# Second mixer's attention as 64-by-64 products on two column halves of TensorE

## The chip, the cores and the metric

The kernel runs on one core of one Trainium2 chip. The metric is the device time of one execution in microseconds. Beside it stands one profiled execution, whose instructions and their times are the trace. Engines are named as the profile does: PE is TensorE's matmuls, PEld its weight loads, DVE is VectorE, ACT is ScalarE, POOL is GpSimd, SP is SyncE, which issues the weight DMAs.

## What is computed

A trunk of two layers over 256 tokens of width 2048, all in float32. Layer 0 has an mLSTM mixer, layer 1 a bidirectional gated linear recurrence (HGRN2), each followed by a ConvGLU block. The change touches the recurrence of layer 1 alone. It has 16 heads of width 128; in one direction, and in chunks of 64 tokens, it is:

```python
def _hgrn_chunk(s_st, xs):
    q, k, lf, v = xs                        # (b, h, 64, 128); lf is the log of the gate
    b = jnp.cumsum(lf, axis=2)
    rel = jnp.where(lower[:, :, None], b[:, :, :, None, :] - b[:, :, None, :, :], -jnp.inf)
    attn = jnp.einsum('bhtsk,bhsk->bhts', jnp.exp(rel) * q[:, :, :, None, :], k)
    o = jnp.einsum('bhts,bhsv->bhtv', attn, v) + jnp.einsum('bhtk,bhkv->bhtv', q * jnp.exp(b), s_st)
    ...
y = hgrn_direction(q, k_f, lf_f, v) + fl(hgrn_direction(fl(q), fl(k_b), fl(lf_b), fl(v)))
```

Written without chunks, the weight of token s in the output at token t is the sum over 128 channels of q[t] k[s] and the product of the gates of all tokens between them, with the forward gates where s is before t and the backward ones where it is after.

## The kernel before

**The stream of weights.** Everything runs under one loop, `stream`, over chunks of weight columns. `split_weights` loads a piece of weights (`raw`), ScalarE rounds it to `wh` (L145), VectorE subtracts the rest into `wl` (L146), and TensorE multiplies: feature-major chunks with weights as the stationary operand (L196 with 512 moving columns, L197 with 256), token-major chunks with the tokens stationary (L186 to L188, 512 columns each). The cast of a piece runs three pieces ahead (`LOOK`). After each step the loop calls `side.tick`, which advances the jobs beside the stream: generators that issue a few instructions and then yield the modelled time until their next turn. The heads of both mixers are such jobs. The order in which the instructions of each engine finally stand is chosen by a scheduler at build time, from this program.

**A head of the second mixer** (`head`, L595 to L656) builds the 256 by 256 matrix of weights between tokens by doubling. `QZ` and `KZ` hold q and k for both directions, with decay applied so far. At level h the tokens form blocks of 2h; within each, the product of the first half's keys with the second half's queries, and the other way round, is a pair (s, t) whose blocks of h differ and whose blocks of 2h agree. Seven levels, h = 1 to 64, cover all pairs within 128 tokens; one more product at the end covers the pairs between the two halves of 128 (L638, L639).

A visit of the job does one level:

- `gather` (L609, `km` and `qm`, four buffers each): VectorE brings the keys and queries that belong to this level into token order.
- L626: two float32 matmuls of 128x128x128 give `pd`, one for each half of the sequence. Only the pairs of this level in it are wanted. L616 is the same for the diagonal, with `ks` and `q`.
- `put` (L604): VectorE copies the wanted pairs with a 0/1 mask of 128 columns out of PSUM into the diagonal blocks of the result `AT`, which POOL has set to zero (L601).
- L627, L628: VectorE multiplies the level's blocks of keys and queries by the gates between them; POOL multiplies neighbouring gates for the next level (L633).

Each visit then yields `SPREAD` = 2.4 (`STEP` = 1.9 in the last two heads). After the last level, L651 multiplies `AT` by the values `V`, ScalarE takes the squares, and the job `finish` scales and transposes the head (L672) for the output projection.

In the first mixer, L393 and L394 transpose four blocks that lie on 64 partitions; the trace shows them as 64*128 where everything else shows 128*128.

Of the kernel before, what the change touches and what calls it, by code (L numbers as in the profile page):

```python
# [8 lines left out]
F32 = mybir.dt.float32  # L9
F32R = mybir.dt.float32r  # L10
I32 = mybir.dt.int32
AF = mybir.ActivationFunctionType
ALU = mybir.AluOpType
PSUM = bass.MemoryType.PSUM

P = 128
T = 256
# [6 lines left out]
BH = 16  # L24
# [15 lines left out]
STEP = 1.9  # L40
SPREAD = 2.4
# [3 lines left out]
MIX = 4  # L45
FIRST = (0, 1, 2, 4, 7, 10, 13, 16)

LEVELS = (1, 2, 4, 8, 16, 32, 64)
C_ID, C_MF, C_MB, C_LV = 0, 128, 384, 640
NCST = C_LV + len(LEVELS) * P  # L50


def trunk_kernel(ctx, tc, xT, pp_d, cst_d, w_first, w_aq, w_ak, w_av, w_ao, w_aout,
                 w_bq, w_bv, w_bg, w_bout, w_up, w_down, out, mscr, stop=9):
    nc = tc.nc
    act, dve, pool, pe = nc.scalar, nc.vector, nc.gpsimd, nc.tensor
# [7 lines left out]
    pp = keep.tile([P, NPP], F32, name="pp")  # L64
    cst = keep.tile([P, NCST], F32, name="cst")
    ones = keep.tile([P, T], F32, name="ones")
# [4 lines left out]
    ident = cst[:, C_ID:C_ID + P]  # L71
# [5 lines left out]
    def aux(name):  # L77
        return psa.tile([P, 512], F32, tag="aux", name=name)
# [132 lines left out]
    def fm_scaled(ps, R, dst, scale=None):  # L211
        fm_sum(ps, dst)
        if scale is None:
            dve.tensor_tensor(dst, dst, R, ALU.mult)
        else:
            dve.scalar_tensor_tensor(dst, dst, scale, R, ALU.mult, ALU.mult)
# [75 lines left out]
    def head_scale(ss, width):  # L292
        rs = ev.tile([P, 2], F32, tag="rs", bufs=6, name="rs")
        dve.tensor_scalar(rs, ss, 1.0 / width, EPS, ALU.mult, ALU.add)
        pool.tensor_tensor(rs, rs, hmx, ALU.pow)
        return rs
# [238 lines left out]
    def hgrn(norm, nxt):  # L535
# [24 lines left out]
        def blocks(z, h, a, b):  # L560
            v = z[:, 0:2 * (T + h)].rearrange("k (p x) -> k p x", p=2)[:, :, a:b]
            return v.rearrange("k p (m j) -> k m p j", j=2 * h)[:, :, :, 0:h]

        def gview(g, n, start, h):
            v = g[:, start:start + 2 * (n - 1)].rearrange("k (p x) -> k p x", p=2)[:, :, 0::2]
            return v.rearrange("k p m -> k m p").unsqueeze(3).broadcast_to([P, n // 2, 2, h])

        def take(hd, what, ps):
            mp = box["mp"]
            st = heads[hd]  # L570
            if what == 0:
                st["q"] = mp.tile([P, T], F32, tag="q", bufs=2, name="q")
                fm_scaled(ps, norm.R, st["q"], box["oml"][:, hd:hd + 1])
                st["QK"] = mp.tile([P, 1152], F32, tag="QK", bufs=2, name="QK")
                st["G"] = mp.tile([P, 768], F32, tag="G0", bufs=2, name="G")
                return
            dr = what - 1
            lb, oml = box["lb"], box["oml"]
            QZ, KZ, G = st["QK"][:, 0:512], st["QK"][:, 512:1024], st["G"]
            z = mp.tile([P, T], F32, tag="z", bufs=2, name="z")  # L580
            fm_scaled(ps, norm.R, z)
            g = G[:, dr * T:(dr + 1) * T]
            kz = KZ[:, dr * T:(dr + 1) * T]
            act.activation(g, z, AF.Sigmoid)
            act.activation(kz, z, AF.Sigmoid, scale=-1.0)
            dve.tensor_scalar(g, g, oml[:, hd:hd + 1], lb[:, hd:hd + 1], ALU.mult, ALU.add)  # L586
            pool.tensor_tensor(QZ[:, (1 - dr) * T:(2 - dr) * T], st["q"], g, ALU.mult)
            if dr == 0:
                pool.tensor_copy(G[:, 512:768], g)
            else:  # L590
                st["ks"] = mp.tile([P, T], F32, tag="ks", bufs=2, name="ks")
                pool.tensor_tensor(st["ks"], KZ[:, 0:T], KZ[:, T:2 * T], ALU.add)
                side.push(head(hd))

        def head(hd):  # L595
            mp = box["mp"]
            st = heads[hd]
            QZ, KZ = st["QK"][:, 0:640], st["QK"][:, 512:1152]
            q, ks, G = st["q"], st["ks"], st["G"]
            AT = mp.tile([P, 4, P], F32, tag="AT", bufs=2, name="AT")  # L600
            pool.memset(AT[:, 0::3], 0.0)  # L601

            def put(ps, mask):
                dve.copy_predicated(AT[:, 0::3], mask.bitcast(I32).unsqueeze(1).broadcast_to([P, 2, P]),  # L604
                                    ps[:, 0:T].rearrange("p (a b) -> p a b", a=2))

            def gather(z, h, tag):
                m = mp.tile([P, T], F32, tag=tag, bufs=MIX, name=tag)
                dve.tensor_copy(m.rearrange("k (m p j) -> k m p j", p=2, j=h), blocks(z, h, 0, T))  # L609
                return m  # L610

            km, qm = gather(KZ, 1, "km"), gather(QZ, 1, "qm")
            pd = aux("pd")
            for t in range(2):
                c = slice(t * P, (t + 1) * P)
                pe.matmul(pd[:, c], ks[:, c], q[:, c], start=True, stop=True)  # L616
            put(pd, ident)
            step = SPREAD if hd < BH - 2 else STEP
            yield step
            n = T  # L620
            for li, h in enumerate(LEVELS):
                pd = aux("pd")
                qa, ka = blocks(QZ, h, 0, T), blocks(KZ, h, 0, T)
                for t in range(2):
                    c = slice(t * P, (t + 1) * P)
                    pe.matmul(pd[:, c], km[:, c], qm[:, c], start=True, stop=True)  # L626
                dve.tensor_tensor(ka, ka, gview(G, n, 1, h), ALU.mult)  # L627
                dve.tensor_tensor(qa, qa, gview(G, n, n + 1, h), ALU.mult)  # L628
                if h < 64:
                    km, qm = gather(KZ, 2 * h, "km"), gather(QZ, 2 * h, "qm")  # L630
                    n //= 2
                    G2 = mp.tile([P, 3 * n], F32, tag=f"G{h}", bufs=2, name="G2")
                    pool.tensor_tensor(G2, G[:, 0:6 * n:2], G[:, 1:6 * n:2], ALU.mult)  # L633
                    G = G2
                put(pd, cst[:, C_LV + li * P:C_LV + (li + 1) * P])
                yield step
            pd = aux("pd")
            pe.matmul(pd[:, 0:P], KZ[:, 0:P], QZ[:, T + P:2 * T], start=True, stop=True)  # L638
            pe.matmul(pd[:, P:T], KZ[:, T + P:2 * T], QZ[:, 0:P], start=True, stop=True)  # L639
            act.copy(AT[:, 1:3], pd[:, 0:T].rearrange("p (a b) -> p a b", a=2))  # L640
            yield
            while "V" not in st["qd"]:
                yield
            V, j = st["qd"]["V"], hd % 4
            py = aux("py")
            y = mp.tile([P, T], F32, tag="y", bufs=4, name="y")
            ss = mp.tile([P, 2], F32, tag="ss", bufs=2, name="ss")
            for t in range(2):
                c = slice(t * P, (t + 1) * P)
                for s in range(2):  # L650
                    pe.matmul(py[:, c], AT[:, 2 * s + t], V[:, s, j * P:(j + 1) * P], start=(s == 0), stop=(s == 1))  # L651
            act.copy(y, py[:, 0:T])
            for t in range(2):
                jk = ev.tile([P, T], F32, tag="jk", bufs=1, name="jk")
                act.activation(jk[:, 0:P], y[:, t * P:(t + 1) * P], AF.Square, accum_out=ss[:, t:t + 1])
            st["y"] = (y, head_scale(ss, 128))  # L656
# [109 lines left out]
    if stop > 1:  # L766
        c, close0 = ffn(0, n1, n2)
        chunks += c
    if stop > 2:
        c = hgrn(n2, n3)  # L770
        b = c[0].before
# [6 lines left out]
    if stop > 3:  # L778
        c, close1 = ffn(1, n3, nf)
# [29 lines left out]
def _constants():  # L809
    c = np.zeros((P, NCST), np.float32)  # L810
    s, t = np.arange(P)[:, None], np.arange(P)[None, :]
    c[:, C_ID:C_ID + P] = s == t
    c[:, C_MF:C_MF + P] = np.where(s > t, BIG, 0.0)
    c[:, C_MB + P:C_MB + 2 * P] = np.where(s < t, BIG, 0.0)
    for i, h in enumerate(LEVELS):
        c[:, C_LV + i * P:C_LV + (i + 1) * P] = (s // (2 * h) == t // (2 * h)) & (s // h != t // h)
    return c


# [53 lines left out]
```

## Time and profile before

| | |
|---|---|
| median of 3 runs | 2469.81 us (2469.35 to 2470.11) |
| the profiled execution's own time | 2469.78 us |
| its span in the trace | 2468.0 us |
| granted TensorE clock, mean | 0.998 |
| second mixer's products, first to last start | 1146.7 to 1646.0 us |
| L626, 448 instructions | 276 ns mean, 66.4 us busy |
| L616, 64 instructions | 274 ns mean |
| L604, 128 masked copies | 436 ns mean, 55.5 us busy |
| POOL memsets of AT (L601), 16 | 314 ns mean |

A row of the groups names line, engine and operation, then output and inputs by the program's names, shapes and count, then busy time and mean duration of one, then the idle time of the engine just before them and what ended it. `128*128` are rows and columns of the array in use. Instructions of TensorE overlap: a duration runs from start to the modelled end, so the pace is read from the starts. One float32 matmul of the program is two weight loads and two matmul instructions in the trace. A timeline row has the start, the duration, the engine, the line and the form, and how many of a kind were merged.

### The profile page before, as it was taken

Reading aid. Unit: us, or ns where it says so; the run is one execution under the profiler, and the core shown is the slowest. Engines: PE = TensorE matmul, PEld = TensorE weight load, DVE = VectorE, ACT = ScalarE, POOL = GpSimd, SP = SyncE. Lnnn points to the kernel's source line nnn. Section 1 sums busy time; section 2 is a strip of 40 time slices with the busy share of each in tenths; the row PEclk is TensorE's granted clock in tenths of the full one; section 3 lists DMA queues with packets and bytes.
Section 4 is the critical chain, followed back from the end, with each engine's and each line's share of the span. In section 5 each row is a group of like instructions: output and inputs, shape, how many; then the busy total and the mean of one; then the engine's idle time right before and its main releaser. Section 6 shows DMA issues by size and latency. Waiting matters only on the chain.

```text
span 2468.0 us, 35972 instructions
## 1 busy us (share of the span) xinstructions
PE 2450.2 (99%) x13950; PEld 2134.1 (86%) x13950; DVE 1781.9 (72%) x2975; ACT 1200.8 (49%) x1810; POOL 272.8 (11%) x341
## 2 busy tenths in 40 slices
PE   9999999999999999999999999999999999999998
PEld 7888888888888888888888888888888888888887
DVE  7766577777656777678888888887777755677754
ACT  6655455444444445444444444445544444444443
POOL 0100032000000000132222222224000000000022
PEclk9999999999999999999999999999999999999999
DMA  7654555666556555555454544446555555666553
GB/s 260 189 178 167 177 183 188 190 189 191 186 189 199 188 188 189 180 194 178 157 168 154 164 161 156 163 145 202 187 189 188 188 188 190 192 192 193 183 190 124
DMA packets 65915, 449.07 MB, mean 182 GB/s; under 512 B 7616, under 2 KB 8128, under 8 KB 15568
## 3 DMA queue, kind: packets, MB, share of 16 engines
q1 hardware_dynamic: 63936, 443.29, 55.4%
q0 software_dynamic: 800, 2.16, 0.6%
q8 instruction: 109, 1.79, 0.3%
q10 hardware_dynamic: 1008, 1.32, 0.1%
q14 instruction: 62, 0.51, 0.1%
HBM read 444.58 MB, written 2.16 MB: 181 GB/s over the span
## 4 chain that ended last, share of the span: by engine, by line
PE 90%; DVE 7%; issue 1%; ACT 1%; DMA 0%; DVEq 0%; POOL 0%; POOLq 0%
PE mm L196 50%; PE mm L197 25%; PE mm L187 3%; PE mm L188 3%; PE mm L186 3%; DVE wl L146 3%; DVE QK L627 1%; PE pd L626 1%; DVE km L609 1%; PE pn L439 1%; PE mm L175 1%; DVE AT L604 1%; PE py L651 1%; DVE qm L609 1%; DVE G L586 0%
## 5 line engine op out<-in xcount | busy, mean ns | idle before, releaser
L146 DVE TENSOR_TENSOR wl<-raw,wh 128x1024 fp32r<-128x1024 f32 (+1 forms) x864 | 1047.1, 1213 | 553.6 <-ACT wh L145 540.6
L145 ACT CAST wh<-raw 128x1024 fp32r<-128x1024 f32 (+1 forms) x864 | 884.4, 1024 | 895.8 <-PE mm L196 500.4
L196 PE MATMUL mm<-xt,wh 128*128 128x512 f32 x3776 | 1318.5, 395 | 0.0
L197 PE MATMUL mm<-xt,wl 128*128 128x256 f32 x3776 | 1050.8, 278 | 0.0
L196 PEld LDWEIGHTS mm<-xt,wh 128*128 128x128 f32 x3776 | 708.0, 188 | 161.2
L197 PEld LDWEIGHTS mm<-xt,wl 128*128 128x128 f32 x3776 | 709.9, 188 | 0.9
L196 PE MATMUL mm<-g,wh 128*128 128x512 f32 x1334 | 462.6, 394 | 0.0
L197 PE MATMUL mm<-g,wl 128*128 128x256 f32 x1334 | 369.5, 277 | 0.0
L196 PEld LDWEIGHTS mm<-g,wh 128*128 128x128 f32 x1334 | 250.1, 188 | 58.1
L197 PEld LDWEIGHTS mm<-g,wl 128*128 128x128 f32 x1334 | 250.4, 188 | 0.0
L186 PE MATMUL mm<-wh,xt 128*128 128x512 f32 x512 | 203.9, 402 | 2.2 <-ACT xt L203 2.2
L187 PE MATMUL mm<-wl,xt 128*128 128x512 f32 x512 | 204.5, 399 | 0.4 <-DVE wl L146 0.4
L188 PE MATMUL mm<-wh,xt 128*128 128x512 f32 x512 | 201.9, 396 | 0.0
L208 ACT COPY b<-mm 128x256 f32<-128x256 f32 x237 | 87.7, 370 | 178.9 <-PE mm L197 178.9
L242 POOL TENSOR_TENSOR acc<-hx 128x256 f32<-128x256 f32 x4 | 4.8, 1205 | 1239.7 <-DVE hx L311 1239.7
L186 PEld LDWEIGHTS mm<-wh,xt 128*128 128x128 f32 x512 | 96.1, 189 | 21.0 <-ACT xt L203 2.5
L187 PEld LDWEIGHTS mm<-wl,xt 128*128 128x128 f32 x512 | 97.0, 189 | 18.4 <-DVE wl L146 0.8
L188 PEld LDWEIGHTS mm<-wh,xt 128*128 128x128 f32 x512 | 97.0, 189 | 18.4
L196 PE MATMUL mm<-yb,wh 128*128 128x512 f32 x256 | 89.6, 396 | 0.0
L196 PE MATMUL mm<-ya,wh 128*128 128x512 f32 x256 | 89.1, 394 | 0.0
L245 POOL TENSOR_TENSOR sq<-hx 128x256 f32<-128x256 f32 x52 | 62.1, 1202 | 197.8 <-DVE hx L311 195.6
L209 DVE TENSOR_TENSOR a<-mm,b 128x256 f32<-128x256 f32 x86 | 36.5, 424 | 51.0 <-ACT b L208 50.9
(185 smaller groups left out, 2083.2 us busy)
## 6 DMA issues: line engine op xcount, KB each, us to landing
raw<-in_w_up SPq DMA_DIRECT2D x172, 1024.0 KB, 5.2
raw<-in_w_down SPq DMA_DIRECT2D x64, 1024.0 KB, 4.9
raw<-in_w_bq SPq DMA_DIRECT2D x48, 1024.0 KB, 5.1
raw<-in_w_ao SPq DMA_DIRECT2D x16, 1024.0 KB, 4.9
raw<-in_w_aout SPq DMA_DIRECT2D x16, 1024.0 KB, 5.2
raw<-in_w_bv SPq DMA_DIRECT2D x16, 1024.0 KB, 4.9
raw<-in_w_bg SPq DMA_DIRECT2D x16, 1024.0 KB, 4.9
raw<-in_w_bout SPq DMA_DIRECT2D x16, 1024.0 KB, 5.1
```

Of the source, the lines that this page charges most:

```text
L145: act.copy(wh[:, :m], r)
L146: dve.tensor_tensor(wl[:, :m], r, wh[:, :m].bitcast(F32), ALU.subtract)
L175: pe.matmul(ps[f][:, 0:T], w[:, c:c + P], x[:, o:o + T], start=(k + kk == 0 and i == 0), stop=(k + kk == ch.nk - 1 and i == 2))
L186: pe.matmul(ps[t], xh, wh[:, c], start=st, stop=False)
L187: pe.matmul(ps[t], xh, wl[:, c], start=False, stop=False)
L188: pe.matmul(ps[t], xl, wh[:, c], start=False, stop=sp)
L196: pe.matmul(ps[f], wh[:, c:c + P], x, start=st, stop=False)
L197: pe.matmul(ps[f][:, 0:T], wl[:, c:c + P], x[:, 0:T], start=False, stop=sp)
L208: act.copy(b, ps[:, T:2 * T])
L209: dve.tensor_tensor(dst, ps[:, 0:T], b, ALU.add)
L245: eng.tensor_tensor(s, hT[k], hT[k], ALU.mult)
L609: dve.tensor_copy(m.rearrange("k (m p j) -> k m p j", p=2, j=h), blocks(z, h, 0, T))
```

## The change

Pairs that a level below 64 wants lie within blocks of 64 tokens, so instead of 128 by 128 products only the 64 by 64 blocks on the diagonal are multiplied: four for each product, on alternating column halves of the array (output partitions 0 to 63 and 64 to 127). At level 64 the queries' block is the neighbouring one (`flip`). The results of the diagonal and of levels 1 to 32 are merged in a packed tile `AD` of 128 partitions by 2 by 64, with masks of 64 columns; at level 64 four ScalarE copies write `AT` from `AD` and from the last product, and the memset of `AT` is gone. A visit now does two products (diagonal and level 1; levels 2 and 4; 8 and 16; 32 and 64) and yields twice the step.

```diff
-LEVELS = (1, 2, 4, 8, 16, 32, 64)
+HALF = 64
+LEVELS = (1, 2, 4, 8, 16, 32, HALF)
-NCST = C_LV + len(LEVELS) * P
+NCST = C_LV + (len(LEVELS) - 1) * HALF
...
-            pool.memset(AT[:, 0::3], 0.0)
-            def put(ps, mask):
-                dve.copy_predicated(AT[:, 0::3], mask.bitcast(I32).unsqueeze(1).broadcast_to([P, 2, P]),
-                                    ps[:, 0:T].rearrange("p (a b) -> p a b", a=2))
+            AD = mp.tile([P, 2, HALF], F32, tag="AD", bufs=2, name="AD")
...
+            def product(pd, k, q, flip=0):
+                for b in range(4):
+                    o, c = b % 2 * HALF, b // 2 * HALF
+                    e = b ^ flip
+                    pe.matmul(pd[o:o + HALF, c:c + HALF], k[:, b * HALF:(b + 1) * HALF], q[:, e * HALF:(e + 1) * HALF],
+                              start=True, stop=True)
...
-            step = SPREAD if hd < BH - 2 else STEP
-            yield step
+            step = 2 * (SPREAD if hd < BH - 2 else STEP)
+            ms = [(gather(KZ, 1, "km"), gather(QZ, 1, "qm"))]
             n = T
-            for li, h in enumerate(LEVELS):
+            for v in range(4):
                 pd = aux("pd")
-                qa, ka = blocks(QZ, h, 0, T), blocks(KZ, h, 0, T)
-                for t in range(2):
-                    c = slice(t * P, (t + 1) * P)
-                    pe.matmul(pd[:, c], km[:, c], qm[:, c], start=True, stop=True)
+                if v == 0:
+                    product(pd[:, 0:P], ks, q)
+                for i, (km, qm) in enumerate(ms):
+                    h = LEVELS[max(0, 2 * v - 1) + i]
+                    w = i if v else 1
+                    product(pd[:, w * P:(w + 1) * P], km, qm, h == HALF)
+                if v == 0:
+                    act.copy(AD, both(pd[:, 0:P]))
+                for i in range(len(ms)):
+                    li = max(0, 2 * v - 1) + i
+                    h = LEVELS[li]
+                    w = i if v else 1
+                    src = both(pd[:, w * P:(w + 1) * P])
+                    if h < HALF:
+                        mask = cst[:, C_LV + li * HALF:C_LV + (li + 1) * HALF].bitcast(I32)
+                        dve.copy_predicated(AD, mask.unsqueeze(1).broadcast_to([P, 2, HALF]), src)
+                    else:
+                        for o in (0, HALF):
+                            act.copy(AT[o:o + HALF, 0::3, HALF - o:P - o], src[o:o + HALF])
+                            act.copy(AT[o:o + HALF, 0::3, o:o + HALF], AD[o:o + HALF])
+                ms = []
+                for h in LEVELS[2 * v:2 * v + 2] if v < 3 else LEVELS[6:]:
...
-                put(pd, cst[:, C_LV + li * P:C_LV + (li + 1) * P])
                 yield step
...
+        same = (s // (2 * h) == t // (2 * h)) & (s // h != t // h)
+        c[:, C_LV + i * HALF:C_LV + (i + 1) * HALF] = same[:, :HALF] | same[:, HALF:]
```

The decays, the gathers and the gates' products stay as they were, now inside the loop over the one or two levels of a visit. The constants' second load shrinks from 896 to 384 columns.

More of the change, by code (lines that the diff above doesn't have):

```diff
@@ L610, in gather @@
                 return m
-            km, qm = gather(KZ, 1, "km"), gather(QZ, 1, "qm")
-            pd = aux("pd")
-            for t in range(2):
-                c = slice(t * P, (t + 1) * P)
-                pe.matmul(pd[:, c], ks[:, c], q[:, c], start=True, stop=True)
-            put(pd, ident)
-            step = SPREAD if hd < BH - 2 else STEP
-            yield step
+            def product(pd, k, q, flip=0):
[4 more added lines that the diff above has]
+                              start=True, stop=True)
@@ L620, in head, with both @@
+            def both(ps):
+                return ps.rearrange("p (a b) -> p a b", a=2)
+            step = 2 * (SPREAD if hd < BH - 2 else STEP)
+            ms = [(gather(KZ, 1, "km"), gather(QZ, 1, "qm"))]
             n = T
-            for li, h in enumerate(LEVELS):
+            for v in range(4):
                 pd = aux("pd")
-                qa, ka = blocks(QZ, h, 0, T), blocks(KZ, h, 0, T)
[L624 to L634, printed above, removed]
-                put(pd, cst[:, C_LV + li * P:C_LV + (li + 1) * P])
+                if v == 0:
[20 more added lines that the diff above has]
+                for h in LEVELS[2 * v:2 * v + 2] if v < 3 else LEVELS[6:]:
+                    qa, ka = blocks(QZ, h, 0, T), blocks(KZ, h, 0, T)
+                    dve.tensor_tensor(ka, ka, gview(G, n, 1, h), ALU.mult)
+                    dve.tensor_tensor(qa, qa, gview(G, n, n + 1, h), ALU.mult)
+                    if h < HALF:
+                        ms.append((gather(KZ, 2 * h, "km"), gather(QZ, 2 * h, "qm")))
+                        n //= 2
+                        G2 = mp.tile([P, 3 * n], F32, tag=f"G{h}", bufs=2, name="G2")
+                        pool.tensor_tensor(G2, G[:, 0:6 * n:2], G[:, 1:6 * n:2], ALU.mult)
+                        G = G2
@@ L814, in _constants @@
     c[:, C_MB + P:C_MB + 2 * P] = np.where(s < t, BIG, 0.0)
-    for i, h in enumerate(LEVELS):
-        c[:, C_LV + i * P:C_LV + (i + 1) * P] = (s // (2 * h) == t // (2 * h)) & (s // h != t // h)
+    for i, h in enumerate(LEVELS[:-1]):
+        same = (s // (2 * h) == t // (2 * h)) & (s // h != t // h)
+        c[:, C_LV + i * HALF:C_LV + (i + 1) * HALF] = same[:, :HALF] | same[:, HALF:]
     return c
```

## The prediction

> **What bounds the kernel now.** I read the page's busy rows first, then the chain that ended last, then the windows of the second mixer, then the forms of the lines that change, and last the timeline around single visits.
>
> ```profile
> PE 2450.2 (99%) x13950; PEld 2134.1 (86%) x13950; DVE 1781.9 (72%) x2975; ACT 1200.8 (49%) x1810; POOL 272.8 (11%) x341
> PE 90%; DVE 7%; issue 1%; ACT 1%; DMA 0%; DVEq 0%; POOL 0%; POOLq 0%
> 1140.00:1660.00 520.00, 517.27 (x2977) 450.25 (x2976) 453.79 (x927) 237.22 (x395) 132.26 (x190) 1.00 0.49 158
> ```
>
> The first two lines are the busy row and the chain's shares; the third is the window in which all products of the second mixer's heads lie. TensorE is busy for 517.27 of 520 us, at a granted clock of 1.00. So the path is TensorE's own stream of instructions: time taken out of it is gained one for one, time put into it is lost one for one. VectorE is the next (453.79, 87%), with idle time left, ScalarE has 46%.
>
> ```profile
> L626 PE MATMUL pd<-qm,km 128*128 128x128 f32 x448 | 66.4, 276 | 2.7 <-DVE qm L609 2.7
> L616 PE MATMUL pd<-q,ks 128*128 128x128 f32 x64 | 9.7, 274 | 0.0
> L604 DVE COPY_PREDICATED AT<-cst,pd 128x256 f32<-128x256 int32 x128 | 55.5, 436 | 0.7
> ...
> 1149.25 0.39 PE L196 MATMUL mm<-xt,wh 128*128 128x512 f32 x1
> 1149.48 0.60 PE L626 MATMUL pd<-qm,km 128*128 128x128 f32 x4
> 1149.84 0.36 PE L197 MATMUL mm<-xt,wl 128*128 128x256 f32 x1
> 1150.04 0.40 PE L196 MATMUL mm<-xt,wh 128*128 128x512 f32 x1
> ```
>
> The counts: 16 heads x (diagonal + 7 levels) = 128 products, each of two matmuls in the program and four instructions in the trace (448 + 64 = 512). Their duration overlaps, so I take starts. In the visit shown, the four begin at 1149.48; the next streamed matmul begins at 1149.84, but lasts 0.36 where its form has 0.28, so 0.08 of it is waiting: it streams from 1149.92. **One product costs 0.444 us** (0.111 per instruction; 75 lone visits have this as their median), and all cost 128 x 0.444 = 56.8 us.
>
> Next, what a tile of less than the full array costs. Before the change it occurs once, in the first mixer's transposes, which use 64 rows (64*128):
>
> ```profile
> 63.44 0.39 PE L188 MATMUL mm<-wh,xt 128*128 128x512 f32 x1
> 63.76 0.14 PEld L393 LDWEIGHTS pt<-cst,C 64*128 64x128 f32 x1 [0.35 <-DVE m L387]
> 63.76 0.27 PE L393 MATMUL pt<-cst,C 64*128 64x64 f32 x1
> 63.96 0.19 PEld L186 LDWEIGHTS mm<-wh,xt 128*128 128x128 f32 x1
> 63.96 0.50 PE L186 MATMUL mm<-wh,xt 128*128 128x512 f32 x1
> ...
> 66.97 0.14 PEld L393 LDWEIGHTS pt<-cst,C 64*128 64x128 f32 x1
> 67.03 0.22 PE L393 MATMUL pt<-cst,C 64*128 64x64 f32 x1
> 67.03 0.14 PEld L394 LDWEIGHTS pt<-cst,m 64*128 64x128 f32 x1
> 67.09 0.22 PE L394 MATMUL pt<-cst,m 64*128 64x64 f32 x1
> ...
> 1257.67 0.28 PE L197 MATMUL mm<-xt,wl 128*128 128x256 f32 x1
> 1257.67 0.26 PEld L672 LDWEIGHTS pz<-cst,y 128*128 128x128 f32 x2
> 1257.79 0.38 PE L672 MATMUL pz<-cst,y 128*128 128x128 f32 x2
> ```
>
> In the ordinary stream, and for the full-array transposes of the last three lines, a weight load starts together with the matmul ahead of it (1257.67 and 1257.67) and is hidden. Into the 64-row tile it starts only at 63.76, 0.32 after the matmul ahead of it, which streams for 0.23: it waited until the array had run empty. The second entry, at 66.91 after a matmul at 66.59, has the same 0.32, so it isn't the wait for m. Out of the tile it is the same: the transpose streams from 63.81 (0.27 where its form has 0.22) and the load of L186 comes 0.15 later, and is then not hidden (0.50 where the form has 0.39).
>
> **The change, part by part.** *Entering and leaving column tiles.* All products become four matmuls of 64 columns on alternating column halves, everything else stays on the full array. So each contiguous group of products in TensorE's order pays one entry and one exit. Entry: load at 0.32, load itself 0.05, against the slot at 0.23: 0.14. Exit: 0.15 until the load, then 0.11 of load in the open, less the 0.06 that the last instruction would have had anyway: 0.20. Together 0.34 us a group. How many groups? The program says two levels a visit, 64 visits; but the order in which the changed kernel's instructions stand has 103 groups: 94 of one product, one of two, eight of four. The scheduler puts each product where its gathered tiles come due, streamed matmuls between. 103 x 0.34 = **35.0 us added**. No row shows a column tile, so the ends are 0 (only row tiles drain) and 35; I take 35, the one row of a partial tile, seen at both of its visits. [...]
>
> *The products.* Each is now eight instructions (four, and each float32 one is two). A 64-column float32 instruction in a partial tile is what the transposes at 66.97 to 67.09 are: 0.06 from start to start. Strictly one after the other, a product takes 8 x 0.06 = 0.48, all 61.4 us. Perfectly side by side, half, 30.7. Neither is seen in this trace. I take a place between: the two instructions of one float32 matmul follow each other on one half and must share it, and only the second of each can run beside the first of the next half: five steps instead of eight, 0.30 a product, **38.4 us** (estimate). The ends stay for the range. [...]
>
> *Masked copies.* 128 of 0.436 on VectorE become 96 of half the elements (0.22 to 0.436): 14 to 35 us less on an engine that isn't the bound. *ScalarE* gets 16 copies of the diagonal and 64 quarter copies at the end, 80 x 0.27 (a 128x128 copy from PSUM took 0.266) = 21 us, on 237 of 520. The quarter copies wait for the last masked copy and the product, and casts of wh are queued behind them; the cast runs three pieces ahead, and a piece lasts eight pairs of 0.23 and 0.12, 2.8 us, so over 8 us cover it. Without the cover it is the 21. The POOL memset of AT goes (16 x 0.31, on an engine with 25%). The late load of the masks shrinks from 896 to 384 columns. All these at nothing; they could only return part of the 2.7 us in which TensorE idles in this window (bound -2.7 to 0).
>
> *Doubled steps.* The visits are half as many and twice as far apart, so a head takes as long as before. Gathers and decays are unchanged in number. A late gather holds the streamed matmuls behind its product, as now (2.7 us, on qm); the four buffers of each gather now hold two visits instead of four.
>
> Sum: -56.8 + 35.0 + 38.4 = **+16.6 us**. The profiled execution took 2469.78 (span 2468.0), the median of the runs is 2469.81, so both give 2486.4.
>
> **The rivals.** (1) *The halves don't run side by side.* Speaking for it: in every row a load starts when the matmul ahead starts, one at a time, so eight loads of 0.05 alone are a chain of 0.43. Against: the halves share no weights and no output partitions. Then -56.8 + 35.0 + 61.4 = +39.6, 2509. (2) *Faster: column halves don't empty the array.* [...] Then entry and exit cost nothing, and with the overlap of five steps -56.8 + 38.4 = -18.4, 2451 (perfectly side by side -26). It decides from a group price of 18.4 / 103 = 0.18 us: under that the kernel gains, over it loses; the row has 0.34. (3) *The change does nothing that counts:* no emptying, but also nothing side by side, 61.4 - 56.8 = +4.6, less up to 2.7 of idle time: within 0.2% (4.9 us, about what measurement of this kernel can tell from no change).
>
> **How the numbers follow.** Forecast case: 0.41; its own range goes from perfect halves less the idle time (-56.8 + 35.0 + 30.7 - 2.7 = +6.2) to halfway between my overlap and none (+28). Rival 1: 0.31. Rival 2: 0.17. Rival 3: 0.11. The emptying stands on a row of this trace that twice shows the same delay, so it gets 0.72; how far the halves overlap stands on none, so that part is split closer to even. The time is that of the forecast case, 2486. The range goes to 2452, where rival 2 begins, and to 2513, over rival 1's 2509; it leaves out about half of rival 2 and a tail above, under 0.2. For the likeliest case alone 2476 to 2498. Faster 0.17, same 0.11, slower 0.72.
>
> **What would show it.** In the changed profile: the first load of a group starting about 0.1 us after the stream ahead has ended (emptying), or together with the matmul ahead of it (rival 2); the first load behind a group 0.15 after the last product instruction; starts of product instructions on the two halves closer than 0.06 (side by side) or evenly 0.06 (rival 1). The group, from the slot to the next streamed matmul, should take about 0.64 instead of 0.444 (0.82 by rival 1, 0.30 by rival 2). TensorE's idle time by DVE should not exceed some 3 us in this window; if it does, or if ScalarE's quarter copies stand ahead of late casts, the forecast is wrong for another reason. A result under 2465 refutes the emptying; one over 2500 refutes the overlap.

## The result and the profile after

The changed kernel takes 2482.61 us (median of 5 runs, 2480.86 to 2482.74) against 2469.81: 12.8 us more, ratio 1.005 (95% interval 1.0035 to 1.0065). Its profiled execution took 2482.74, its span is 2480.9, 12.9 more than before. The forecast was 2486 and slower.

In the changed kernel the stream's lines are one number higher (L197 and L198 for L196 and L197); L614 is the product, L606 the gather, L640 the masked copy, L632 ScalarE's copy of the diagonal, L643 and L644 its quarter copies. Page and window first, then the groups, with the same columns as before:

```profile
PE 2461.8 (99%) x14462; PEld 2114.1 (85%) x14462; DVE 1762.4 (71%) x2943; ACT 1221.2 (49%) x1890; POOL 273.6 (11%) x325
...
1140.00:1680.00 540.00, 536.09 (x3536) 437.14 (x3535) 440.02 (x904) 262.47 (x482) 136.03 (x178) 1.00 0.46 155
```

```profile
L614 PE MATMUL pd<-qm,km 128*64 128x64 f32 x896 | 49.6, 234 | 3.9 <-DVE qm L606 3.8
L640 DVE COPY_PREDICATED AD<-cst,pd 128x128 f32<-128x128 int32 x96 | 27.4, 292 | 3.1 <-PE pd L614 2.9
L643 ACT COPY AT<-pd 64x128 f32<-64x128 f32 x32 | 8.3, 258 | 16.1 <-DVE AD L640 15.9
L644 ACT COPY AT<-AD 64x128 f32<-64x128 f32 x32 | 9.5, 297 | 0.2
L614 PE MATMUL pd<-q,ks 128*64 128x64 f32 x128 | 7.2, 234 | 0.0
L632 ACT COPY AD<-pd 128x128 f32<-128x128 f32 x16 | 4.3, 266 | 42.0 <-PE pd L614 42.0
```

TensorE is still the bound (536.09 of 540 us, clock 1.00). There are 1024 product instructions for 512, in the form 128*64: all rows, half of the columns. The busy time of the products fell (49.6 + 7.2 for 66.4 + 9.7), and yet the kernel is longer: the loss stands between the instructions. VectorE is relieved of 28.1 us of masked copies (55.5 to 27.4), ScalarE has 22.1 us more (8.3 + 9.5 + 4.3); TensorE waits for neither (its matmuls' waits in this window are 3.8 us, all for `qm`). The timeline of one group of a single product shows where the time went:

```profile
1148.27 0.28 PE L198 MATMUL mm<-xt,wl 128*128 128x256 f32 x1
1148.27 0.19 PEld L197 LDWEIGHTS mm<-xt,wh 128*128 128x128 f32 x1
1148.39 0.40 PE L197 MATMUL mm<-xt,wh 128*128 128x512 f32 x1
1148.71 0.31 PEld L614 LDWEIGHTS pd<-qm,km 128*64 128x64 f32 x8 [0.25 <-DVE qm L606]
1148.71 0.45 PE L614 MATMUL pd<-qm,km 128*64 128x64 f32 x8
1149.09 0.19 PEld L198 LDWEIGHTS mm<-xt,wl 128*128 128x128 f32 x1
1149.10 0.39 PE L198 MATMUL mm<-xt,wl 128*128 128x256 f32 x1
```

In the stream a load starts with the matmul ahead of it (both 1148.27). The first load of the product starts only at 1148.71, 0.326 us after the start of a matmul that streams for 0.231, so 0.095 after it ended; the 0.25 that the row puts down to `qm` is this emptying, for the first experiment below pays the same where `qm` was already in use. Behind the product the first load comes at 1149.09, 0.150 after the last product instruction (1148.944), and is not hidden: the matmul lasts 0.39 where its form has 0.28. Within the group the eight starts are, in ns after 1148000: 714 and 721, 821 and 827, 879 and 886, 937 and 944: pairs 7 ns apart, the second pair 107 ns behind the first, then one every 58 ns.

I count a group from slot to slot: from the moment at which the streamed matmul ahead of it has streamed to the one at which the next begins to. Such a group takes 0.579 us (median of 76). The one group of two takes 0.808, so a second product adds 0.229 to 0.231, four steps of 0.058. **A group's price is 0.579 - 4 x 0.058 = 0.347, a product's 0.231.**

I split the stage from layer 0's last down-projection matmul to layer 1's first. Every streamed matmul counts at its usual distance (0.231, 0.1156 or 0.228), 800.8 us in all kernels; the products with their waits are what stands between streamed matmuls besides; of the rest, each excess up to 25 ns is *pace*, and larger ones are *other stalls*. The last column goes from the stage's end to the start of TensorE's last matmul.

| us | stage | products and waits | pace | other stalls | behind the stage |
|---|---|---|---|---|---|
| before | 865.8 | 61.6 | 2.5 | 0.9 | 476.1 |
| after | 879.3 | 72.2 | 5.2 | 1.0 | 476.1 |

That is +13.5, and 0.7 less ahead of the stage. The clean sums, at these prices and without waits, are 56.8 before, and 103 x 0.347 + 128 x 0.231 = 65.3 after: +8.5 is the change itself, +2.1 waits for gathers, +2.7 pace.

One short stretch hides behind the 1.00 of the window above. In the first group of four TensorE waits twice for `qm`, 0.9 us each (1165.4 to 1167.4 us), and from 1167.4 to 1170.8 the granted clock is 0.50: streamed 512-column matmuls stand 0.427 us apart there instead of 0.231. The kernel before has one wait of 1.4 us and no such stretch. Half of 3.4 us, 1.7, is the most that it can cost (an estimate); the columns don't hold it apart.

### The profile page after: what moved, and what is told of

The parts are those of the page before. It is cut to its first block, busy times and chain, and to the rows that moved or that the text cites. A ratio compares the mean times of both kernels' runs of the same rounds, so it can differ in the third digit from the quotient of the medians.

```text
span 2480.9 us, 37013 instructions
## 1 busy us (share of the span) xinstructions
PE 2461.8 (99%) x14462; PEld 2114.1 (85%) x14462; DVE 1762.4 (71%) x2943; ACT 1221.2 (49%) x1890; POOL 273.6 (11%) x325
## 4 chain that ended last, share of the span: by engine, by line
PE 96%; DVE 2%; ACT 1%; issue 0%; DMA 0%; SPq 0%; DVEq 0%; POOL 0%; ACTq 0%; POOLq 0%
PE mm L197 52%; PE mm L198 26%; PE mm L189 4%; PE mm L188 4%; PE mm L187 4%; PE pd L614 2%; DVE wl L147 1%; PE pn L440 1%; PE py L671 1%; PE mm L176 1%; DVE QK L648 0%; ACT wh L146 0%; PE S L426 0%; DVE qm L606 0%; DMA raw<-in_w_first 0%
## 5 line engine op out<-in xcount | busy, mean ns | idle before, releaser
L197 PE MATMUL mm<-xt,wh 128*128 128x512 f32 x3776 | 1319.6, 395 | 0.0
L146 ACT CAST wh<-raw 128x1024 fp32r<-128x1024 f32 (+1 forms) x864 | 884.3, 1024 | 854.9 <-PE mm L197 476.6
L198 PE MATMUL mm<-xt,wl 128*128 128x256 f32 x3776 | 1050.7, 278 | 0.0
L197 PEld LDWEIGHTS mm<-xt,wh 128*128 128x128 f32 x3776 | 708.0, 188 | 163.7
L198 PEld LDWEIGHTS mm<-xt,wl 128*128 128x128 f32 x3776 | 710.0, 188 | 1.2
L197 PE MATMUL mm<-g,wh 128*128 128x512 f32 x1334 | 462.6, 394 | 0.0
L198 PE MATMUL mm<-g,wl 128*128 128x256 f32 x1334 | 369.5, 277 | 0.0
L197 PEld LDWEIGHTS mm<-g,wh 128*128 128x128 f32 x1334 | 250.1, 188 | 58.1
L198 PEld LDWEIGHTS mm<-g,wl 128*128 128x128 f32 x1334 | 250.4, 188 | 0.0
L197 PE MATMUL mm<-yb,wh 128*128 128x512 f32 x256 | 90.6, 399 | 0.0
L197 PE MATMUL mm<-ya,wh 128*128 128x512 f32 x256 | 89.1, 394 | 0.0
```

The lines of the kernel that those rows point to most:

```text
L146: act.copy(wh[:, :m], r)
L197: pe.matmul(ps[f], wh[:, c:c + P], x, start=st, stop=False)
L198: pe.matmul(ps[f][:, 0:T], wl[:, c:c + P], x[:, 0:T], start=False, stop=sp)
```

## The experiments

All were timed in five rounds beside the kernel before, whose median was 2469.1 to 2469.6 in them. `pin` below stands for keeping TensorE's instructions in the order of the program.

| kernel | groups | time, us | ratio (95%) | products and waits | pace | other stalls | behind the stage |
|---|---|---|---|---|---|---|---|
| before + unread pair | 112 | 2517.39 | 1.0194 (1.0180 to 1.0208) | 109.2 | 3.3 | 0.1 | 476.1 |
| halves apart | 104 | 2482.04 | 1.0053 (1.0040 to 1.0065) | 71.3 | 5.3 | 1.7 | 476.1 |
| before, two levels a visit | none | 2469.39 | 1.0000 (0.9991 to 1.0009) | 60.6 | 4.1 | 0.2 | 476.5 |
| two levels, in order | 50 | 2565.44 | 1.0389 (1.0375 to 1.0404) | 115.6 | 5.0 | 40.2 | 476.5 |
| twos, later | 57 | 2488.18 | 1.0078 (1.0066 to 1.0091) | 52.2 | 9.5 | 12.8 | 484.9 |
| fours | 32 | 2526.67 | 1.0232 (1.0218 to 1.0246) | 95.0 | 5.9 | 21.6 | 476.1 |
| fours, full products | none | 2538.91 | 1.0284 (1.0270 to 1.0298) | 118.1 | 3.1 | 13.2 | 476.1 |
| twos, pinned later | 57 | 2481.21 | 1.0044 (1.0032 to 1.0057) | 54.1 | 8.5 | 2.8 | 484.9 |
| twos, full products | none | 2481.70 | 1.0047 (1.0034 to 1.0059) | 67.2 | 4.3 | 5.0 | 476.1 |
| fours, pinned later | 32 | 2515.72 | 1.0190 (1.0176 to 1.0203) | 95.5 | 6.1 | 8.8 | 476.5 |
| twos, nudged | 57 | 2471.70 | 1.0010 (1.0001 to 1.0019) | 54.0 | 7.1 | 2.9 | 476.1 |

Groups are runs of column-half instructions in TensorE's order.

**The emptying by itself.** The kernel before, with one pair of products on the column halves behind each level's full product; nobody reads it.

```diff
                     pe.matmul(pd[:, c], km[:, c], qm[:, c], start=True, stop=True)
+                for o in (0, 64):
+                    pe.matmul(pd[o:o + 64, T:T + 64], km[:, o:o + 64], qm[:, o:o + 64], start=True, stop=True)
```

> The kernel before with one unread pair of 64-column products (one on each half) behind each of the 112 products of a level; TensorE's order has them as 112 groups of their own. Theory (entering and leaving column tiles empties the array): a group costs 0.35 (a lone group of the changed kernel, 0.579 from slot to slot, less four steps of 0.058) and two steps of 0.058, 0.46; 112 x 0.46 = 52 us more than before, 2522. Rival (a column tile costs its steps alone, and the changed kernel lost its time to waits): two to four steps of 0.058, 13 to 26 us more, 2483 to 2496.

```profile
L628 PE MATMUL pd<-qm,km 128*64 128x64 f32 x448 | 37.6, 246 | 0.0
```

The 448 instructions form 112 groups of four, each 0.464 from slot to slot (median; 51.9 in all): 0.347 and two steps of 0.058 make 0.463. The kernel got 47.9 us longer, less than the 51.9, since some 4 us of the waits went in the shadow of the pairs (the idle time ahead of L626's loads is 11.8 us in the kernel before, 8.0 here). So the price belongs to the pair of changes from full array to column halves and back, not to anything else in the changed kernel.

**Do the halves need alternating instructions?** The changed kernel with the blocks of one half written together, then those of the other.

```diff
-                for b in range(4):
+                for b in (0, 2, 1, 3):
```

> The changed kernel, each product's four blocks in the order first half, first half, second half, second half. Theory A (only instructions that are neighbours in the program run side by side): instead of four steps of 0.058 a product takes about seven, 0.41; 128 x 0.175 = 22 us more than the changed kernel, 2505. Theory B (each half takes its own instructions from those that are waiting, as the starts 0.007 apart suggest): the same as the changed kernel, 2481 to 2484.

A lone group took 0.586 instead of 0.579, the kernel as long as the changed one (the intervals lie on each other). The starts come in pairs still, now 13 ns apart every 58. The wider pairs show that the order did change, and that they are pairs shows that the other half's first instruction doesn't wait for the four ahead of it: each half takes its own.

**Visits and steps alone.** The kernel before with two levels a visit and doubled steps, its full products, masks and memset kept.

```diff
-            step = SPREAD if hd < BH - 2 else STEP
+            step = 2 * (SPREAD if hd < BH - 2 else STEP)
+            ms = [(gather(KZ, 1, "km"), gather(QZ, 1, "qm"))]
...
+            for v in range(4):
+                pd = aux("pd")
+                if v == 0:
+                    product(pd[:, 0:T], ks, q)
+                for i, (km, qm) in enumerate(ms):
+                    w = i if v else 1
+                    product(pd[:, w * T:(w + 1) * T], km, qm)
```

> The kernel before with two levels a visit and doubled steps as in the changed kernel, but full 128 by 128 products and full masks. Theory (the visits themselves cost nothing): 2467 to 2473, as before. Rival (a part of the 13 us is the visits' schedule): 2474 to 2480.

No difference (ratio 1.0000). The visits and doubled steps, which the prediction put at nothing, are nothing, and the +12.8 belong to the halves and what comes with them (masks, copies, order).

**Fewer groups, by order alone.** If a group costs 0.347 and a product gains 0.444 - 0.231 = 0.213, the change breaks even at 128 x 0.213 / 0.347 = 78 groups. The changed kernel with the stream and the products of the second mixer pinned, and the first product one step later:

```diff
-                            pe.matmul(ps[f], wh[:, c:c + P], x, start=st, stop=False)
+                            pin(pe.matmul(ps[f], wh[:, c:c + P], x, start=st, stop=False))
...
             ms = [(gather(KZ, 1, "km"), gather(QZ, 1, "qm"))]
+            yield SPREAD
```

> The changed kernel with the streamed matmuls and the products of the second mixer kept in the program's order on TensorE, and the first gather of a head one step ahead of its product. TensorE's order then has 50 groups (36 of two products, 14 of four) instead of 103. Theory (a group costs 0.35 whatever its size): 53 x 0.347 = 18 us less than the changed kernel, 2464, faster than before by 6. Rival (waits and the schedule are what the change lost to): products that must keep their place wait for their gathers in the stream, 2483 or more.

The 50 groups came, clean they would be 50 x 0.347 + 29.6 = 47.0 us, and yet it lost 96.0. The list of waits (what waited for what: us in total, times, longest) names the reason, a window what came with it:

```profile
PE pd L620 <- DVE qm L612: 47.2, 16, 3.2
PE pd L620 <- POOL ks L599: 10.1, 8, 1.7
```

```profile
1150.00:1250.00 100.00, 89.34 (x568) 74.23 (x568) 71.14 (x145) 41.20 (x75) 21.06 (x32) 0.91 0.40 135
```

Sixteen times the product stood in TensorE's queue before its gather was there, with the whole stream behind it. The granted clock of the window is 0.91: after two waits of 1.2 and 2.8 us between 1174.0 and 1178.4, streamed 512-column matmuls stand 0.43 apart instead of 0.23. By their distances, 27 of this kernel's 40.2 us of other stalls are streamed matmuls at half clock. (In the changed kernel the stretch at 0.50 came behind two waits of 0.9.) The rival (waits) was right. This order had let one level's products follow their gathers too closely, so the next kernels do one level a step, collect the products in a list, and issue them together. In the groups of two a head's first products also come two steps later (`for _ in range(2)` below), in the groups of four not:

```diff
+            due = [(-1, ks, q)]
+            km, qm = gather(KZ, 1, "km"), gather(QZ, 1, "qm")
+            for _ in range(2):
+                yield step
...
+                due.append((li, km, qm))
...
+                if len(due) == GROUP:
...
+                    for ps, (l, k, qq) in zip(out, due):
+                        product(ps, k, qq, l == len(LEVELS) - 1)
```

Groups of two (`GROUP` = 2):

> As the kernel kept in order before (e3_in_order), but a head gathers and decays one level a step, its first product comes two steps later, and two products are issued together once their gathers are a step old. TensorE's order has 57 groups (50 of two products, seven of four). Theory (a group costs 0.347 whatever its size, a product 0.231, and what e3_in_order lost were the 3 us waits of each head's first products for their gathers): 57 x 0.347 + 128 x 0.231 - 56.8 = -7.4 against the kernel before, and up to 5 less if its waits go too: 2457 to 2464. Rival (keeping products in their place makes TensorE wait for VectorE whatever the distance): 2500 or more.

The products with their waits fell to 52.2 us, 9.4 less than before: right. The kernel still lost, for two other reasons. From 1116.2 to 1122.9 us TensorE waited in the norm, whose matmuls the pinned stream could no longer pass, and the granted clock was 0.50 from 1118.2 to 1128.3:

```profile
PE pc L260 <- DVE acc L254: 6.7, 1, 6.7
```

And from about 1664 us to the end the stream ran at another pace (below), which cost 8.8 us behind the stage.

Groups of four (`GROUP` = 4, five buffers of each gather for four), and the same order with full products (and one buffer less for the heads' results, for room):

> The same with four products together (diagonal and levels 1, 2, 4; then levels 8 to 64), five buffers for the gathers: 32 groups. Theory: 32 x 0.347 + 128 x 0.231 - 56.8 = -16.1 against the kernel before, and up to 5 less: 2448 to 2454. Rival (waits): 2500 or more; a group price that grows with the size of the group: 2460 or more.

> The control for e4_fours: the same visits of four products, the same order kept on TensorE, but full 128 by 128 products and full masks as before the change (and three instead of four buffers for y, for room). Theory (column tiles bring the difference, order alone only the waits of the kernel before, 5 us): 2464 to 2470. Rival (what e4_fours gains is the order): as e4_fours, within 4 us.

The window of the heads in the groups of four:

```profile
1140.00:1680.00 540.00, 498.94 (x3331) 422.55 (x3330) 418.20 (x845) 244.21 (x445) 136.51 (x169) 0.96 0.44 147
```

Both lost much: in the products' column 95.0 - 40.7 (clean) = 54 us and 118.1 - 56.8 = 61. In the groups of four 37.6 us are TensorE's waits for `qm` by the profile (36.8 in the control); the clock comes on top. If it was either 1.00 or 0.50, as in the trace of the changed kernel, 0.96 over 540 us is some 43 us at 0.50, which costs 22 at most (an estimate). The control has 0.96 too, where the kernel before and the groups of two have 1.00. Neither expectation of the control came: it is not at 2464 to 2470, nor within 4 us of the groups of four. With the same order the halves are 23.1 us better than the full products in this column, and 12.2 in time; the order itself is what costs.

**The same, pinned only from the first head on.** The groups of two, their control with full products, and the groups of four with seven buffers of each gather (and single ones of two small tiles, for room). The line moves from the second mixer's set-up into the head:

```diff
-            in_order.append(1)
...
+            in_order.append(1)
```

> e8_twos_late, with TensorE's order kept only from the first head on. In e8_twos_late it was kept from the mixer's first chunk, and the streamed matmuls had to stand behind the norm's small products, which cost 9 us of waiting at 1123 to 1126 us; also its streamed pairs ran at 0.353 instead of 0.347 from 1620 us to the end, 16 us for the part behind the second mixer's products. Theory (57 groups x 0.347 + 128 x 0.231 = 49.4 instead of 61.6 with its waits before): without the 9 us, 2478 if the slower pace stays, 2459 to 2463 if it doesn't. Rival (products kept in place always cost waits): as e8_twos_late, 2485 or more.

> The control for e9_twos: same visits, same kept order, full 128 by 128 products and full masks. Theory: 128 x 0.444 = 56.8 and none of the 5 us of waits before: 2463 to 2467 at the faster pace, so 4 to 8 over e9_twos at equal pace. Rival (what e9_twos gains is the order alone): within 2 us of e9_twos at equal pace.

> e4_fours with the order kept only from the first head on, and seven instead of five buffers for the gathers (room from single buffers for z and the smaller gates' tiles): seven waits of 4.4 us, one for each pair of heads that run at once, should go with the buffers, 9 us with the norm. Theory: 32 x 0.347 + 128 x 0.231 = 40.7 instead of 61.6: 2449 to 2455, up to 16 more if the slower pace holds. Rival (the gathers come too late for groups of four whatever the buffers): 2500 or more.

The products in the groups of two, then in their control:

```profile
L622 PE MATMUL pd<-qm,km 128*64 128x64 f32 x896 | 39.9, 228 | 3.7 <-DVE qm L614 3.7
```

```profile
L625 PE MATMUL pd<-qm,km 128*128 128x128 f32 x448 | 63.0, 279 | 6.3 <-DVE qm L617 6.2
```

With groups of two the halves take 54.1 us and full products in the same order 67.2: 13.1 less (7.4 of it clean, 56.8 - 57 x 0.347 - 29.6; the rest are waits that the control has and this has not, among them one of 3.5 us with 3.4 us at a clock of 0.50 behind it). The control had been expected to have no waits; it has 10.4 us over its clean 56.8. Against the kernel before the groups of two are 7.5 less, as the two prices say. So column halves do gain in this column once their groups are few. The time didn't show it, 2481.21 and 2481.70: against the kernel before, 6.0 us more of pace in the stage and 8.8 behind it ate the gain. The groups of four again stood waiting:

```profile
1236.93 0.92 PE L622 MATMUL pd<-qm,km 128*64 128x64 f32 x24
1242.20 0.45 PE L622 MATMUL pd<-qm,km 128*64 128x64 f32 x8 [4.35 <-DVE qm L614]
```

Three products of the group run, the fourth's `qm` (level 64) is 4.35 us late, for on VectorE it stands behind another head's work: copies and decays of levels 1 and 2, and one `wl` of 1.40, run from 1236.8 us on, its own copy at 1241.7 (levels by the access patterns of the trace). More buffers don't change that order (the waits for `qm` are 37.3 us with seven, 37.6 with five); the rival was right.

**The pace.** Four streamed matmuls (512, 256, 512, 256 columns) take either 693.3 or 706.6 ns, at the same granted clock. Behind the stage, the kernel after and the groups of two differ in nothing that they issue:

```profile
1900.00:2300.00 400.00, 400.00 (x2310) 349.65 (x2309) 267.89 (x407) 188.36 (x265) 0.00 (x0) 1.00 0.57 190
```

```profile
1900.00:2300.00 400.00, 400.00 (x2266) 347.00 (x2265) 261.53 (x396) 185.50 (x260) 0.00 (x0) 1.00 0.55 187
```

TensorE is busy for all of the 400 us in both, at clock 1.00, with 2310 matmuls in the changed kernel (first line) and 2266 in the groups of two (second), 1.9% fewer. The last kernel is the groups of two, with the stream of the last block interrupted four times, by one, two, three and four matmuls of one column that nobody reads:

```diff
+        def nudge(count):
+            def go():
+                t = aux("nudge")
+                for _ in range(count):
+                    tc.keep_in_program_order(pe.matmul(t[:, 0:1], ones[:, 0:P], ones[:, 0:1], start=True, stop=True))
+            return go
+        for i, count in ((2, 1), (4, 2), (6, 3), (8, 4)):
+            c[i].before = nudge(count)
```

> The kernel of two products a group pinned from the first head on, and in the last block four short interruptions of the stream: one, two, three and four float32 matmuls of one column on the full array (nobody reads them) ahead of its chunks 2, 4, 6 and 8. The question is the pace of the stream: four streamed matmuls (512, 256, 512, 256 columns) take 693.3 or 706.6 ns at the same granted clock, and that kernel took 706.6 from about 1560 us to its end. Theory A: the pace is a state in which two periodic trains of work stand to each other, kept until the stream is interrupted, so it changes only at a nudge or at the norms' matmuls, and stays as it was left. If one of the first two nudges leaves it at 693.3, most of the 8.8 us come back: 2471 to 2475; if each flips it, about half: 2475 to 2479. Theory B: the pace comes from something that goes on there (transfers, the work of the other engines), and the nudges change nothing: 2481 to 2484, with 706.6 ns through the last block.

```profile
1803.82 0.72 PE L816 MATMUL nudge<-ones 128*128 128x1 f32 x6
...
1900.00:2300.00 400.00, 400.00 (x2310) 349.80 (x2309) 267.23 (x405) 189.10 (x265) 0.00 (x0) 1.00 0.57 190
```

The pace was 706.6 up to the first nudge (1757.9), stayed so behind it and behind the second (1780.8), was 693.3 directly behind the third (1803.8), and stayed 693.3 behind the fourth (1826.7) to the end. In the changed kernel the pace went from 706.6 to 693.3 at the norm's matmuls (1760 to 1766 us); the same matmuls of the groups of two (1743 to 1749) left it at 706.6. So theory A holds as far as it goes: the pace is kept over hundreds of periods and changes at an interruption, though not at every one. The other engines' work goes on across the third nudge (ScalarE's cast from 1803.95 lasts 1.05 us), and in the changed kernel the DMA share is 0.57 at 706.6 (1690 to 1755 us) and 0.58 at 693.3 (1770 to 1835): nothing here shows that transfers or the other engines set the pace by themselves. The time fell from 2481.21 to 2471.70, within the 2471 to 2475 expected, though that had been for a switch at the first or second nudge. It doesn't beat the kernel before (1.0010, interval 1.0001 to 1.0019): the 7.6 us that its products save go to 4.6 us of pace in the stage, 2.0 of stalls, and 2.2 of nudges, of which one switched it.

## Why the prediction was right, step by step

- *Bound.* TensorE's stream sets the time, one for one: the stage's 13.5 us, less the 0.7 ahead of it, are the span's 12.9 but for rounding.
- *Entering and leaving.* 0.34 a group predicted, 0.347 measured, and 103 groups; 35.7 us for 35.0. A group of one takes 0.579 where 0.64 was forecast, the difference being the product. The load 0.095 behind the end of the stream, and 0.150 behind the last product instruction, are as foreseen. The row tile of the first mixer was the right row for column tiles: its first load comes 0.32 behind the start of the matmul ahead, the load of the stream 0.15 behind its transpose, where the column halves have 0.326 and 0.150; the unread pairs, with 0.464 a group, pay the same 0.347. Rival 2 (no emptying) fell with it.
- *Products.* This term was mis-sized: 0.30 predicted, 0.231 measured, 8.8 us too much (38.4 for 29.6). What failed is the argument that the two instructions of one float32 matmul must follow each other before the other half can start. The halves run fully side by side (four steps of 0.058 for eight instructions), at the end that I had called perfect, and don't even need alternating instructions (0.586 for 0.579 a lone group). Rival 1 (one after the other) is refuted by starts 7 ns apart (its chain of eight loads of 0.05 is 0.40, not 0.43; no sum uses it).
- *Copies, visits, steps.* At nothing, and nothing: two levels a visit alone gave 1.0000, ScalarE's 22.1 us (21 predicted) delay no cast that TensorE waits for (from 1140 to 1680 us no matmul waits for `wh`).
- *Waits.* -2.7 to 0 was given; they rose by 2.1. The row of L614 has 3.8 us of idle time by `qm`, over the 3 that I had set as a bound. The eight groups of four would take 0.347 + 4 x 0.231 = 1.27 us clean; they take 2.02 in the median, for the last of their gathers. The fall of the clock behind two such waits (3.4 us at 0.50) was not foreseen either.
- *Pace.* +2.7 in the stage, not foreseen by any step.

So the sum came out as -56.8 + 35.7 + 29.6 = +8.5, with +2.1 and +2.7 that it didn't have and -0.7 ahead of the stage: 2482.4, where 2482.6 was measured and 2486 forecast. That the time lies so near is in part luck: the products' term was 8.8 us too large, and 4.8 us of waits and pace that the sum didn't have made up for more than half of it. The sign rested on the emptying alone, and at 0.347 a group it was over the 78 groups at which it turns.

## What to carry to other kernels

Half tiles of the array paid per change of shape here, not per product: count the contiguous groups in the engine's final order (here 0.35 us each) against what the smaller products save (0.213 each), before counting instructions. Making groups larger by holding TensorE to an order moves the cost into waits, for each product must then be ready when its group is (37.6 us of waits for `qm` in the groups of four), and the granted clock was lower beside them (0.96 over the window of the groups of four); two a group was still worth it here (54.1 us of products and waits for 61.6 before), four was not (95.0). On an engine that is full, measure the pace of the undisturbed stream as well: here it moved by as much as the change did (6.0 us in the stage and 8.8 behind it in the groups of two, against the change's 12.8).

## What was not expected of the hardware

- Column halves of float32 products run fully side by side, pairs 7 ns apart (13 with one half's instructions written first), a step of 0.058 us for both.
- The stream has two paces at the same granted clock, 693.3 and 706.6 ns for four matmuls, kept until an interruption: three one-column matmuls switched it, one and two did not (in the one profiled execution). Within 693.3 the distances repeat every four matmuls (231, 113, 232, 118 ns), within 706.6 every six (236, 113, 232, 118, 241, 120). What two things stand to each other in it, and which interruption switches it, stays open; so does whether a kernel of groups of two at 693.3 throughout the stage would beat the kernel before (an estimate from the table, 7.5 us less of products and 1.9 more of stalls, says some 5 us; not run).
- Short waits came ahead of a halved clock: two of 0.9 us within 2 us were followed by 3.4 us at a granted clock of 0.50 (the changed kernel), and one of 3.5 as well (the control of the groups of two); a single one of 1.4 (the kernel before) or 1.7 (the groups of two) was not. What decides between them stays open.
